# Values' projection partly accumulated beside the keys' in the opening stage, and the recurrence's head arrays split by token chunk

## The chip, the cores and the metric

The kernel runs on one core of a Trainium2 chip. The time is that of one execution in device microseconds, and the number to compare is the median of a few runs. Five engines run their own instruction queues in order: PE multiplies matrices, DVE, ACT and POOL work on vectors, SP issues transfers. They wait for each other through semaphores.

## What is computed

Two layers of a trunk over 128 context tokens and 1024 latent tokens, 1152 columns in all, with model width 1024.

```python
# every sub-layer: h = x*(1+scale)+shift ; x <- LayerNorm(ALPHA*x + gate*sublayer(h))
def _modulation(cond, w_mod, b_mod):
    return jnp.split(jax.nn.silu(cond) @ w_mod + b_mod, 6, axis=-1)
...
def _attn_conv_project(h, w_in, q_gain, k_gain):
    q, k, v, bg, cg, xi = jnp.split(h @ w_in, EVEN_SPLITS, axis=-1)
    ...
# layer 0: attention (8 query heads, 2 key/value heads) beside
    sc = bg * _dwconv(cg * xi, conv_w)
    return jnp.concatenate([att, sc], axis=-1) @ w_out, k, v
# layer 1: HGRN, 8 heads, per direction and head
def _chunk_scan(q, log_f, k, v, s0):
    ...
        decay = jnp.exp(jnp.where(lower, diff, -jnp.inf))
        scores = jnp.einsum('bhtk,bhsk,bhtsk->bhts', qb, kb, decay)
    ...
# after each of the two: a gated ConvFFN
    u = _dwconv(h @ w_up, conv_w); a, gt = jnp.split(u, 2, axis=-1)
    return (jax.nn.silu(gt) * a) @ w_down
```

## The kernel before, in words

Tokens stand on the free axis in three chunks c = 2, 1, 0 of 384 columns (386 or 388 with the halo). A product of full precision is three matmuls on split operands (`mm3`, L93 to L95: hi·hi, hi·lo, lo·hi).

**Opening stage (L341 to L475).** For each of eight blocks b of the model width, `modulation(b)` loads w_mod (`mr`), ACT and DVE split it (L396, L397), 16 matmuls (L403) fill a small bank `psr`, and DVE writes shift and scale (L412, L414). `modulate(b)` transposes x (L421, banks `psx`), DVE applies shift and scale (`ht`, L424), ACT and POOL split it into `hT` (L427, L428), and nine matmuls per chunk group add block b to the keys' projection in `psk`, three banks. The banks of `psr` and `psx` come from one pool of five.

**Features of attention (L545 on).** j = 4 are the keys, j = 5 the values, j = 0 to 3 the queries. `feature` loads a 512 KB weight and runs 72 matmuls into three banks. ACT copies the banks to `fT` (L549), PE transposes `fT` into token order (L558).

**Conv stage (L617 to L641).** Twelve features f0 to f11, three to each j: cg (ACT), xi times cg (`pr`, DVE L630), bg times the convolution (`sc`, DVE L639). Two triples of PSUM banks take turns, so a feature's first matmul waits until the feature two before it has been read. Between these, DVE adds up the rest of the modulation from w_mod (`macc`, L170 and L172, four instructions to each 512 KB load `mraw`; the ring holds two loads), PE transposes the sums (`mps`), DVE reduces them (L183, L184), and `gate_store` (L235) writes the finished gate `gd` to DRAM from SP's queue.

In these stages a scheduler that simulates the kernel's time line picks the order of each engine's instructions. From the out projection of layer 0 on, the order is as written.

**Recurrence (L1500 to L1720).** For each of eight heads, the tile X holds four arrays of 1152 columns. Its items run over levels lv = 0 to 6 and within each over c = 2, 1, 0. `mixed_keys(lv, c)` copies interleaved halves of X into `km` on ACT (L1624). `level(lv, c)` multiplies `km` by X on PE (L1635), and then POOL and DVE each scale one half of X in place (L1641). The queue of PE puts three or six matmuls of the next head's projections between two items. The last head, from 2268 us on, has less to put there.

Of the kernel before, what the change touches and what calls it, by code (L numbers as in the profile page):

```python
# [80 lines left out]
def build(tc, ins, outs, consts):  # L81
# [263 lines left out]
    def bank(name):  # L345
        return pd.tile([P, 512], F32, tag="d", name=name)

    with ExitStack() as st:
        pd = st.enter_context(tc.tile_pool(name="pdS", reuse_waits="tile", bufs=5, space=PSUM))
        sp = st.enter_context(tc.tile_pool(name="sp", reuse_waits="tile", bufs=1))  # L350
# [33 lines left out]

        psk = pu.tile([P, 3, 512], F32, tag="u", name="psu")
        wm = ins["w_mod"][0].rearrange("(k p) (j f) -> p k j f", p=P, j=6)
        def modulation(b):
# [28 lines left out]
        def modulate(b):  # L416
# [12 lines left out]
            for c in (2, 1, 0):  # L429
                a = 1 + c * OW  # L430
                mm3(psk[:, c, :OW], (wkey[0][:, b, :], wkey[1][:, b, :]), (hT[0].k(b, a, OW), hT[1].k(b, a, OW)),
                    b == 0, b == KT - 1)

        modulation(0)
        load_x(0)
        wkey = wload(wcols(w_in, 512), KT, P)
        for b in range(KT):
            if b + 1 < KT:
                modulation(b + 1)
            if b % 2 == 0 and b < 6:  # L440
                load_x(b // 2 + 1)
            modulate(b)
# [56 lines left out]
    with ExitStack() as st:  # L499
        wk = st.enter_context(tc.tile_pool(name="wk", reuse_waits="tile", bufs=1))  # L500
        st.enter_context(qk)
        pus = [st.enter_context(tc.tile_pool(name="puA2", reuse_waits="tile", bufs=1, space=PSUM)), pu]
        pd = st.enter_context(tc.tile_pool(name="pdA", reuse_waits="tile", bufs=2, space=PSUM))
# [42 lines left out]
        for j in (4, 5, 0, 1, 2, 3):  # L546
            ps = psk if j == 4 else feature(pus[(j + 1) % 2], j * P, OW, 1)
            fT = work([P, SW], "fT")
            nc.scalar.activation(fT.rearrange("p (a b) -> p a b", b=OW), ps[:, :, :OW], AF.Copy)  # L549
            if j == 4:  # L550
# [925 lines left out]
    def first_split(n):  # L1476
# [15 lines left out]
    masks = gs.tile([P, 7, P], U8, name="masks")  # L1492
    m32 = gp.tile([P, 4, NTOK], I32, tag="X", name="m32").rearrange("p a b -> p (a b)")[:, :7 * P].rearrange(
        "p (a b) -> p a b", b=P)
# [32 lines left out]
    def scan_ap(X, a0, a1, c0, n, h):  # L1527

        base = X[:, a0, c0:c0 + n]
        return bass.AP(base.tensor, base.offset,  # L1530
                       [list(base.ap[0]), [2 * h, n // (2 * h)], [(a1 - a0) * NTOK + h, 2], [1, h]])

# [6 lines left out]
    class Head:  # L1539
# [42 lines left out]
        def begin(self):  # L1582
            self.X = persistent("X", [P, 4, NTOK])
            self.sT = persistent("sT", [P, NT, P])
            self.T128 = gp.tile([P, 2, NT], F32, tag="T128", bufs=2, name="T128")
            self.tots = {}
# [5 lines left out]
        def arrays(self, c):  # L1592
            X, fb, q, cols = self.X, self.fb, self.q[c], colsof(c)
            nc.scalar.activation(X[:, 0:4:3, cols], fb[:, :, cols], AF.Identity, bias=one, scale=-1.0)
            nc.gpsimd.tensor_tensor(X[:, QAF, cols], q, fb[:, 0, cols], op=ALU.mult)
            nc.vector.tensor_tensor(X[:, QAB, cols], q, fb[:, 1, cols], op=ALU.mult)
            kk = self.kk[c] = wtile("kk")
            nc.vector.tensor_tensor(kk, X[:, KBF, cols], X[:, KBB, cols], op=ALU.add)

# [21 lines left out]
        def mixed_keys(self, lv, c):  # L1621
            km = self.km[lv, c] = wtile("km")
            hh = 1 << lv
            nc.scalar.copy(km.rearrange("p (n s r) -> p n s r", s=2, r=hh),  # L1624
                           scan_ap(self.X, KBF, KBB, c * 384, 384, hh))

        def level(self, lv, c):
            X, cols = self.X, colsof(c)
            hh = 1 << lv
# [3 lines left out]
            for q3 in range(3):  # L1633
                c0 = c * 384 + q3 * P
                mm(ps[:, q3 * P:(q3 + 1) * P], km[:, q3 * P:(q3 + 1) * P], scan_ap(X, QAB, QAF, c0, P, hh),  # L1635
                   start=True, stop=True)
            t4 = self.tots[c][lv].rearrange("p a (n s) -> p a n s", s=2)
            for half, arrs in ((0, slice(0, 2)), (1, slice(2, 4))):
                x = X[:, arrs, cols].rearrange("p a (n s r) -> p a n s r", s=2, r=hh)[:, :, :, half, :]
                eng = nc.vector if half else nc.gpsimd  # L1640
# [6 lines left out]
        def state_at(self, dr, t):  # L1647
            if t == (8 if dr else 1):
                return self.S0[:, dr, :]
            return self.X[:, KBB if dr else KBF, t * P:(t + 1) * P]  # L1650

        def flip(self, dr, c):
            pt = pmt()
            for q3 in range(3):
                t = 3 * c + q3
                nc.tensor.transpose(pt[:, q3 * P:(q3 + 1) * P],
                                    self.X[:, KBB if dr else KBF, t * P:(t + 1) * P], ident)
            kb = wtile("kb")
# [21 lines left out]
        def output(self, c):  # L1680
            po = pst()
            X, V = self.X, shared["V"]
            for q3 in range(3):
                t = 3 * c + q3
                cols = slice(t * P, (t + 1) * P)
                o = po[:, q3 * P:(q3 + 1) * P]
# [438 lines left out]
```

## Time and profile before

| what | value |
|---|---|
| median of 3 runs | 3256.94 us (3255.2 to 3258.32) |
| the profiled execution | 3256.72 us, span 3254.9 us |
| PE busy in the span | 3136.4 us, 96% |
| DVE, POOL, ACT busy | 2247.9, 1422.9, 1288.9 us |

The span is what the trace covers. The time of the execution is 1.8 us longer. PE is the busiest engine, and its idle time is 3254.9 − 3136.4 = 118.5 us.

### The profile page before, as it was taken

To read this page: it belongs to the slowest core of one execution; us is meant where nothing else is said; L and a number is where in the kernel's file an instruction comes from. 1 tells how busy PE (TensorE), PEld (TensorE's weight loads), DVE (VectorE), ACT (ScalarE), POOL (GpSimd) and SP (SyncE) were. 2 spreads that over 40 slices of the span, in tenths; PEclk is the share of its full clock that TensorE was granted. 3 is DMA by queue.
4 is the path that set the end of the run, shared out by engine and by line. 5 is a ranking of instruction groups with operands and counts; after the bars stand their busy time and mean duration, and the time that the engine had idled before them with its cause. 6 is when DMAs were issued, how large, how long until landed. Compare 5 with 4: busy or idle time off the path is not lost. (4 is left out here: it accounts for less than half of the span.)

```text
span 3254.9 us, 48740 instructions
## 1 busy us (share of the span) xinstructions
PE 3136.4 (96%) x19231; PEld 2906.1 (89%) x19231; DVE 2247.9 (69%) x3117; ACT 1288.9 (40%) x2162; POOL 1422.9 (44%) x1011
## 2 busy tenths in 40 slices
PE   7999999899999999998999999999999999999997
PEld 5999888789999998877999999999779999998886
DVE  6778888448988976674466666655556889675356
ACT  4411998333333333115433334333443433335112
POOL 6821242335444534562244333333424545444465
PEclk9999999999999999999999999999999999999999
DMA  7142000322222335541322222211331222225452
GB/s 221 35 136 91 1 1 1 129 85 67 95 91 88 91 119 188 171 154 64 99 83 76 65 68 80 62 50 43 111 122 55 87 91 91 69 82 185 154 169 83
DMA packets 267476, 305.42 MB, mean 94 GB/s; under 512 B 19587, under 2 KB 200015, under 8 KB 267248
## 3 DMA queue, kind: packets, MB, share of 16 engines
q1 hardware_dynamic: 266160, 299.49, 29.0%
q8 instruction: 152, 2.49, 0.3%
q0 software_dynamic: 1088, 2.82, 0.3%
q14 instruction: 76, 0.62, 0.1%
HBM read 237.84 MB, written 64.42 MB: 93 GB/s over the span
## 5 line engine op out<-in xcount | busy, mean ns | idle before, releaser
L1099 POOL TENSOR_TENSOR wlo<-S,whi 128x512 fp32r<-128x512 f32 x152 | 243.1, 1613 | 251.9 <-ACT whi L1098 251.3
L109 POOL TENSOR_TENSOR wlo<-wraw,whi 128x1024 fp32r<-128x1024 f32 x78 | 198.0, 2541 | 203.4 <-ACT whi L108 203.2
L93 PE MATMUL psd<-whi,s 128*128 128x512 f32 x720 | 284.0, 394 | 0.9 <-DVE u L1243 0.9
L95 PE MATMUL psd<-whi,s 128*128 128x512 f32 x720 | 284.0, 394 | 0.0
L94 PE MATMUL psd<-wlo,s 128*128 128x512 f32 x720 | 284.0, 394 | 0.0
L1641 POOL TENSOR_TENSOR X<-X,tot 128x384 f32<-128x384 f32 x144 | 181.4, 1260 | 226.8 <-PE pss L1635 173.7
L1127 DVE SCALAR_TENSOR_TENSOR t<-u,fcw,t 128x1156 f32<-128x1156 f32 x152 | 266.2, 1768 | 13.5 <-ACT t L1122 10.8
L95 PE MATMUL psq<-T,wlo 128*128 128x290 f32 x912 | 271.0, 297 | 0.0
L94 PE MATMUL psq<-T,whi 128*128 128x290 f32 x912 | 270.5, 297 | 0.0
L93 PE MATMUL psq<-T,whi 128*128 128x290 f32 x912 | 270.3, 296 | 0.0
L1099 POOL TENSOR_TENSOR wlo<-wraw,whi 128x512 fp32r<-128x512 f32 x114 | 182.2, 1599 | 173.1 <-ACT whi L1098 157.3
L108 ACT ACTIVATE whi<-wraw 128x1024 fp32r<-128x1024 f32 x130 | 136.8, 1054 | 291.2 <-DMA wraw<-in_ffn_w_down_dram 107.0
L1098 ACT ACTIVATE whi<-S 128x512 fp32r<-128x512 f32 x152 | 92.9, 627 | 323.2 <-DVE S L1077 249.0
L1357 DVE TENSOR_TENSOR y<-y,psd 128x512 f32<-128x512 f32 x144 | 98.0, 684 | 171.9 <-PE psd L95 171.3
L213 DVE SCALAR_TENSOR_TENSOR macc<-mraw,sil,macc 128x512 f32<-128x512 f32 x182 | 191.7, 1092 | 7.1 <-DMA mraw<-in_w_mod_dram 7.1
L93 PE MATMUL psu<-h,whi 128*128 128x388 f32 (+1 forms) x504 | 175.0, 348 | 12.1 <-DVE sc L639 6.9
L1641 DVE TENSOR_TENSOR X<-X,tot 128x384 f32<-128x384 f32 x144 | 102.1, 709 | 113.1 <-PE pss L1635 75.1
L94 PE MATMUL psu<-h,whi 128*128 128x388 f32 (+1 forms) x504 | 174.4, 346 | 2.5 <-POOL h L428 2.5
L1635 PE MATMUL pss<-X,km 128*128 128x128 f32 x1008 | 153.2, 289 | 23.7 <-ACT km L1624 10.3
L93 PE MATMUL psp<-s,whi 128*128 128x384 f32 x480 | 174.7, 364 | 0.0
L95 PE MATMUL psu<-h,wlo 128*128 128x388 f32 (+1 forms) x504 | 173.2, 344 | 0.0
L94 PEld LDWEIGHTS psq<-T,whi 128*128 128x128 f32 x912 | 172.5, 189 | 0.0
(442 smaller groups left out, 10005.2 us busy)
## 6 DMA issues: line engine op xcount, KB each, us to landing
wraw<-in_ffn_w_up_dram SPq DMA_DIRECT2D x88, 512.0 KB, 3.8
mraw<-in_w_mod_dram SPq DMA_DIRECT2D x104, 256.0 KB, 2.8
sraw<-sd SPq DMA_DIRECT2D x40, 578.0 KB, 4.6
wraw<-in_ffn_w_down_dram SPq DMA_DIRECT2D x44, 512.0 KB, 4.1
sd<-t SPq DMA_DIRECT2D x36, 578.0 KB, 3.0
wraw<-in_hgrn_w_in_dram SPq DMA_DIRECT2D x40, 512.0 KB, 4.1
mraw<-in_w_mod_dram SPq DMA_DIRECT2D x28, 512.0 KB, 4.0
wraw<-in_attn_w_in_dram SPq DMA_DIRECT2D x18, 512.0 KB, 3.8
```

Source lines behind the costliest of these rows:

```text
L93: mm(ps, l[0], r[0], start=start, stop=False)
L94: mm(ps, l[0], r[1], start=False, stop=False)
L95: mm(ps, l[1], r[0], start=False, stop=stop)
L108: nc.scalar.activation(hi[:, :n], raw[:, :n], AF.Copy)
L109: (eng or nc.gpsimd).tensor_tensor(lo[:, :n], raw[:, :n], r32(hi[:, :n]), op=ALU.subtract)
L213: nc.vector.scalar_tensor_tensor(acc[:, cond, :], raw, sil[:, cond, k:k + 1], acc[:, cond, :], op0=ALU.mult, op1=ALU.add)
L1098: nc.scalar.activation(hi, src, AF.Copy)
L1099: nc.gpsimd.tensor_tensor(lo, src, r32(hi), op=ALU.subtract)
L1127: nc.vector.scalar_tensor_tensor(t, u[:, :, c0:c0 + HO], taps(p + NF * x)[c0], t, op0=ALU.mult, op1=ALU.add)
L1357: nc.vector.tensor_tensor(y[t][:, cols], y[t][:, cols], ps, op=ALU.add)
L1635: mm(ps[:, q3 * P:(q3 + 1) * P], km[:, q3 * P:(q3 + 1) * P], scan_ap(X, QAB, QAF, c0, P, hh), start=True, stop=True)
L1641: eng.tensor_tensor(x, x, t4[:, :, :, 1 - half].unsqueeze(3).to_broadcast([P, 2, nb, hh]), op=ALU.mult)
```

## The change

Three things are edited. First, `wval`, the values' weight, is loaded right behind the keys', and for every block b the values' chunks 2 and 1 (six matmuls of 386 columns, 48 over the eight blocks) are added up in two banks `psv` of a pool of their own. The feature j = 5 then does chunk 0 alone, 24 matmuls, and ACT copies `psv` to `fTv` ahead of it. Second, the pool of `psr` and `psx` goes from five banks to three, which makes room for the two. Third, X becomes three tiles X0, X1, X2 of 384 columns. No engine gains or loses an instruction except ACT, which has one more.

```diff
+    qv = ExitStack()
+    pv = qv.enter_context(tc.tile_pool(name="puV", reuse_waits="tile", bufs=1, space=PSUM))
     with ExitStack() as st:
-        pd = st.enter_context(tc.tile_pool(name="pdS", reuse_waits="tile", bufs=5, space=PSUM))
+        pd = st.enter_context(tc.tile_pool(name="pdS", reuse_waits="tile", bufs=3, space=PSUM))
...
         psk = pu.tile([P, 3, 512], F32, tag="u", name="psu")
+        psv = pv.tile([P, 2, 512], F32, tag="v", name="psv")
...
                 mm3(psk[:, c, :OW], (wkey[0][:, b, :], wkey[1][:, b, :]), (hT[0].k(b, a, OW), hT[1].k(b, a, OW)),
                     b == 0, b == KT - 1)
+            for c in (2, 1):
+                a = 1 + c * OW
+                mm3(psv[:, c - 1, :OW], (wval[0][:, b, :], wval[1][:, b, :]), (hT[0].k(b, a, OW), hT[1].k(b, a, OW)),
+                    b == 0, b == KT - 1)
...
         wkey = wload(wcols(w_in, 512), KT, P)
+        wval = wload(wcols(w_in, 640), KT, P)
...
+        fTv = wk.tile([P, SW], F32, tag="fT", bufs=2, name="fT")
+        nc.scalar.activation(fTv[:, OW:].rearrange("p (a b) -> p a b", b=OW), psv[:, :, :OW], AF.Copy)
+        qv.close()
         pus = [st.enter_context(tc.tile_pool(name="puA2", reuse_waits="tile", bufs=1, space=PSUM)), pu]
...
-            ps = psk if j == 4 else feature(pus[(j + 1) % 2], j * P, OW, 1)
-            fT = work([P, SW], "fT")
-            nc.scalar.activation(fT.rearrange("p (a b) -> p a b", b=OW), ps[:, :, :OW], AF.Copy)
+            if j == 5:
+                ps, fT = pus[0].tile([P, 3, 512], F32, tag="u", name="psu"), fTv
+                for k in range(KT):
+                    mm3(ps[:, 0, :OW], (wval[0][:, k, :], wval[1][:, k, :]),
+                        (hT[0].k(k, 1, OW), hT[1].k(k, 1, OW)), k == 0, k == KT - 1)
+                nc.scalar.activation(fT[:, :OW], ps[:, 0, :OW], AF.Copy)
+            else:
+                ps = psk if j == 4 else feature(pus[(j + 1) % 2], j * P, OW, 1)
+                fT = work([P, SW], "fT")
+                nc.scalar.activation(fT.rearrange("p (a b) -> p a b", b=OW), ps[:, :, :OW], AF.Copy)
...
-            self.X = persistent("X", [P, 4, NTOK])
+            self.X = [persistent(f"X{c}", [P, 4, 384]) for c in range(3)]
...
             nc.scalar.copy(km.rearrange("p (n s r) -> p n s r", s=2, r=hh),
-                           scan_ap(self.X, KBF, KBB, c * 384, 384, hh))
+                           scan_ap(self.X[c], KBF, KBB, 0, 384, hh))
...
-                mm(ps[:, q3 * P:(q3 + 1) * P], km[:, q3 * P:(q3 + 1) * P], scan_ap(X, QAB, QAF, c0, P, hh),
+                mm(ps[:, q3 * P:(q3 + 1) * P], km[:, q3 * P:(q3 + 1) * P], scan_ap(X, QAB, QAF, q3 * P, P, hh),
                    start=True, stop=True)
...
-                x = X[:, arrs, cols].rearrange("p a (n s r) -> p a n s r", s=2, r=hh)[:, :, :, half, :]
+                x = X[:, arrs, :].rearrange("p a (n s r) -> p a n s r", s=2, r=hh)[:, :, :, half, :]
```

The change also moves rows that it does not name. The order is shown at three places, as the built programs have it.

**PE at the end of the opening stage, before.** `psu_132` is the keys' bank group, and `psu_859` that of the values' feature j = 5, which PE mixes with the keys' last block.

```order
L94 MATMUL psu_859<-h11_95,whi_855 128x386
L95 MATMUL psu_859<-h01_93,wlo_856 128x386
L94 MATMUL psu_132<-h11_95,whi_176 128x386
L95 MATMUL psu_132<-h01_93,wlo_177 128x386
L93 MATMUL psu_132<-h01_93,whi_176 128x386
L93 MATMUL psu_859<-h00_92,whi_855 128x386
L94 MATMUL psu_859<-h10_94,whi_855 128x386
L95 MATMUL psu_859<-h00_92,wlo_856 128x386
L94 MATMUL psu_132<-h11_95,whi_176 128x386
L95 MATMUL psu_132<-h01_93,wlo_177 128x386
L93 MATMUL psu_859<-h00_92,whi_855 128x386
L94 MATMUL psu_859<-h10_94,whi_855 128x386
```

The same place after the change: `psu_135` is the keys', `psv_136` the values' two banks, `psu_914` the values' chunk 0.

```order
L95 MATMUL psv_136<-h01_93,wlo_187 128x386
L93 MATMUL psv_136<-h01_93,whi_186 128x386
L94 MATMUL psu_135<-h11_95,whi_180 128x386
L95 MATMUL psu_135<-h01_93,wlo_181 128x386
L93 MATMUL psu_135<-h01_93,whi_180 128x386
L94 MATMUL psv_136<-h11_95,whi_186 128x386
L95 MATMUL psv_136<-h01_93,wlo_187 128x386
L94 MATMUL psu_135<-h11_95,whi_180 128x386
L95 MATMUL psu_135<-h01_93,wlo_181 128x386
L93 MATMUL psu_914<-h00_92,whi_186 128x386
L94 MATMUL psu_914<-h10_94,whi_186 128x386
L95 MATMUL psu_914<-h00_92,wlo_187 128x386
```

The values' chunks now run through all eight blocks, and their chunk 0 starts only when the last matmul into `psv` has been issued.

**DVE in the conv stage around the second `sc`, before.** `pr` opens the stretch, and L184 is what `gate_store` waits for.

```order
L630 TENSOR_TENSOR pr<-psu,cg 128x1164
L183 TENSOR_REDUCE mods<-mps 128x4 x2
L170 TENSOR_SCALAR macc<-mraw,sil 128x512 x2
L184 TENSOR_TENSOR mods<-mods,colA 128x4 x2
L633 SCALAR_TENSOR_TENSOR yv<-pr,colB,yv 128x1158
L172 SCALAR_TENSOR_TENSOR macc<-mraw,sil,macc 128x512 x2
L634 SCALAR_TENSOR_TENSOR yv<-pr,colB,yv 128x1158
L172 SCALAR_TENSOR_TENSOR macc<-mraw,sil,macc 128x512 x8
L639 TENSOR_TENSOR sc_1676<-psu,yv 128x1158
L172 SCALAR_TENSOR_TENSOR macc<-mraw,sil,macc 128x512 x4
```

After the change the reduction L183 and L184 stands further down among the sums:

```order
L183 TENSOR_REDUCE mods<-mps 128x4 x2
L172 SCALAR_TENSOR_TENSOR macc<-mraw,sil,macc 128x512
L170 TENSOR_SCALAR macc<-mraw,sil 128x512
L172 SCALAR_TENSOR_TENSOR macc<-mraw,sil,macc 128x512
L651 SCALAR_TENSOR_TENSOR yv<-pr,colB,yv 128x1158
L170 TENSOR_SCALAR macc<-mraw,sil 128x512
L184 TENSOR_TENSOR mods<-mods,colA 128x4 x2
L172 SCALAR_TENSOR_TENSOR macc<-mraw,sil,macc 128x512
L652 SCALAR_TENSOR_TENSOR yv<-pr,colB,yv 128x1158
L172 SCALAR_TENSOR_TENSOR macc<-mraw,sil,macc 128x512 x5
L657 TENSOR_TENSOR sc_1682<-psu,yv 128x1158
L172 SCALAR_TENSOR_TENSOR macc<-mraw,sil,macc 128x512 x8
```

From the stage's start, the second `sc` has 60 instructions of `macc` ahead of it before and 56 after, which is 15 and 14 loads.

**SP in the same stretch, before.** The first row here issues loads 11 to 14.

```order
L160 DMA mraw<-in_w_mod_dram 128x2x512 x4
L100 DMA wraw<-in_attn_w_in_dram 128x8x128
L235 DMA gd_83<-mods 128x8x1 x2
L160 DMA mraw<-in_w_mod_dram 128x2x512 x3
L100 DMA wraw<-in_attn_w_in_dram 128x8x128
```

After the change the first row issues loads 10 to 13, and load 14 is the single one below it.

```order
L160 DMA mraw<-in_w_mod_dram 128x2x512 x4
L100 DMA wraw<-in_attn_w_in_dram 128x8x128
L160 DMA mraw<-in_w_mod_dram 128x2x512
L235 DMA gd_83<-mods 128x8x1 x2
L160 DMA mraw<-in_w_mod_dram 128x2x512 x2
L100 DMA wraw<-in_attn_w_in_dram 128x8x128
L160 DMA mraw<-in_w_mod_dram 128x2x512 x2
```

In both orders 14 loads stand ahead of `gd`. The load that the second `sc` needs last was behind `gd` and is now ahead of it.

**PE in the last head of the recurrence, before.** These are the level matmuls with the semaphores that they wait for; rows of other matmuls between them are left out.

```order
L1635 MATMUL pss_20908<-X_14568,km_20894 128x128 [waits Pool_49]
L1635 MATMUL pss_20908<-X_14568,km_20894 128x128 x2
L1635 MATMUL pss_20920<-X_14568,km_20906 128x128 [waits Pool_49]
L1635 MATMUL pss_20920<-X_14568,km_20906 128x128 x2
L1635 MATMUL pss_20937<-X_14568,km_20918 128x128 [waits DVE_49]
L1635 MATMUL pss_20937<-X_14568,km_20918 128x128 x2
```

After the change:

```order
L1652 MATMUL pss_20916<-X1_14575,km_20902 128x128 [waits Activation_49]
L1652 MATMUL pss_20916<-X1_14575,km_20902 128x128 x2
L1652 MATMUL pss_20928<-X0_14574,km_20914 128x128 [waits Activation_49]
L1652 MATMUL pss_20928<-X0_14574,km_20914 128x128 x2
L1652 MATMUL pss_20945<-X2_14576,km_20926 128x128 [waits Activation_49]
L1652 MATMUL pss_20945<-X2_14576,km_20926 128x128 x2
```

The order is the same. Each group waits for ACT alone, where it waited for POOL's or DVE's update of X by the item before it, which belongs to another chunk.

## Rows read from the trace of the kernel before

**Rows 1.** The page, each engine's busy us, share of the span, instructions.

```profile
PE 3136.4 (96%) x19231; PEld 2906.1 (89%) x19231; DVE 2247.9 (69%) x3117; ACT 1288.9 (40%) x2162; POOL 1422.9 (44%) x1011
```

**Rows 2.** Windows: length, busy us of PE, PEld, DVE, ACT, POOL, PEclk, DMA, GB/s.

```profile
17.70:53.60 35.90, 28.87 (x177) 20.87 (x177) 26.61 (x40) 20.84 (x35) 20.82 (x19) 0.95 1.13 315
53.60:83.00 29.40, 29.04 (x189) 26.81 (x190) 19.53 (x48) 14.08 (x30) 21.82 (x30) 1.00 0.28 79
...
238.50:262.10 23.60, 16.69 (x82) 16.44 (x81) 18.34 (x29) 2.11 (x3) 2.34 (x1) 0.78 0.66 193
...
2268.00:2312.00 44.00, 35.22 (x219) 31.09 (x219) 30.31 (x51) 17.07 (x32) 26.64 (x21) 0.96 0.29 89
```

**Rows 3.** PE's waits in the whole span: total us, times, longest.

```profile
PE pss L1635 <- ACT km L1624: 10.3, 11, 1.2
PE pss L1635 <- POOL X L1641: 9.7, 14, 1.7
PE psu L93 <- DVE sc L639: 6.9, 1, 6.9
PE psr L403 <- ACT mhi L396: 6.8, 4, 3.2
...
PE psu L94 <- POOL h L428: 2.5, 4, 1.5
...
PE pss L1635 <- DVE X L1641: 2.1, 6, 0.5
...
PE psu L93 <- DVE pr L630: 2.0, 1, 2.0
```

**Rows 4.** PE's time line: first and last of 28 matmul starts of j = 5.

```profile
75.02 0.33 PE L93 MATMUL psu<-h,whi 128*128 128x386 f32 x1
...
79.77 0.34 PE L93 MATMUL psu<-h,whi 128*128 128x386 f32 x1
```

**Rows 5.** ACT's time line: the keys' copy out of PSUM.

```profile
75.48 1.12 ACT L549 ACTIVATE fT<-psu 128x1158 f32<-128x1158 f32 x1
```

**Rows 6.** DVE's time line: the last block's four `ht`.

```profile
65.60 2.03 DVE L424 TENSOR_SCALAR ht<-psx,s,mods 128x384 f32<-128x384 f32 x4
```

**Rows 7.** DMA issues from 0 to 70 us: count, KB each, median us to landing.

```profile
wraw<-in_attn_w_in_dram SPq DMA_DIRECT2D x5, 512.0 KB, 6.5
```

**Rows 8.** PE's time line in the conv stage: the features f6 and f7 start.

```profile
225.46 0.45 PE L93 MATMUL psu<-h,whi 128*128 128x388 f32 x1 [2.00 <-DVE pr L630]
...
246.28 0.66 PE L93 MATMUL psu<-h,whi 128*128 128x388 f32 x1 [6.91 <-DVE sc L639]
```

**Rows 9.** Windows of the features f7 and f8, columns as in Rows 2.

```profile
246.20:262.10 15.90, 15.82 (x74) 15.81 (x75) 14.25 (x24) 0.13 (x1) 0.00 (x0) 0.80 0.75 229
262.70:275.60 12.90, 12.90 (x76) 12.90 (x75) 12.87 (x19) 1.63 (x3) 3.08 (x2) 1.00 0.33 102
```

**Rows 10.** DVE's time line in the conv stage ahead of the second `sc`.

```profile
228.79 3.54 DVE L172 SCALAR_TENSOR_TENSOR macc<-mraw,sil,macc 128x512 f32<-128x512 f32 x2
...
242.12 2.74 DVE L172 SCALAR_TENSOR_TENSOR macc<-mraw,sil,macc 128x512 f32<-128x512 f32 x4 [5.80 <-DMA mraw<-in_w_mod_dram]
244.78 1.35 DVE L639 TENSOR_TENSOR sc<-psu,yv 128x1158 f32<-128x1158 f32 x1
```

**Rows 11.** DMA issues from 160 to 275 us, columns as in Rows 7.

```profile
mraw<-in_w_mod_dram SPq DMA_DIRECT2D x24, 512.0 KB, 4.0
...
gd<-mods SPq DMA_DIRECT2D x2, 4.0 KB, 10.9
```

**Rows 12.** PE's time line: the first level matmul of the second head.

```profile
1677.72 1.25 PE L1635 MATMUL pss<-X,km 128*128 128x128 f32 x6 [1.15 <-ACT km L1624]
```

**Rows 13.** POOL's time line, one update of X in the last head.

```profile
2284.91 1.28 POOL L1641 TENSOR_TENSOR X<-X,tot 128x384 f32<-128x384 f32 x1 [0.62 <-ACT km L1624]
```

**Rows 14.** PE's time line behind that update.

```profile
2286.25 0.94 PE L1635 MATMUL pss<-X,km 128*128 128x128 f32 x6 [1.26 <-POOL X L1641]
```

**Rows 15.** POOL's groups by shape in the last head, 2268 to 2312 us.

```profile
L1641 POOL TENSOR_TENSOR X<-X,tot 128x384 f32<-128x384 f32 x18 | 22.4, 1244 | 11.8 <-PE pss L1635 6.9 <-ACT km L1624 4.1 <-ACT h L1727 0.6
```

More of the change, by code (lines that the diff above doesn't have):

```diff
@@ L1492, in build @@
     masks = gs.tile([P, 7, P], U8, name="masks")
-    m32 = gp.tile([P, 4, NTOK], I32, tag="X", name="m32").rearrange("p a b -> p (a b)")[:, :7 * P].rearrange(
+    m32 = gp.tile([P, 4, 384], I32, tag="X0", name="m32").rearrange("p a b -> p (a b)")[:, :7 * P].rearrange(
         "p (a b) -> p a b", b=P)
@@ L1530, in scan_ap @@
         return bass.AP(base.tensor, base.offset,
-                       [list(base.ap[0]), [2 * h, n // (2 * h)], [(a1 - a0) * NTOK + h, 2], [1, h]])
+                       [list(base.ap[0]), [2 * h, n // (2 * h)], [(a1 - a0) * 384 + h, 2], [1, h]])
     def colsof(c):
@@ L1592, in arrays @@
         def arrays(self, c):
[L1593 to L1596, printed above, removed]
+            X, fb, q, cols = self.X[c], self.fb, self.q[c], colsof(c)
+            nc.scalar.activation(X[:, 0:4:3, :], fb[:, :, cols], AF.Identity, bias=one, scale=-1.0)
+            nc.gpsimd.tensor_tensor(X[:, QAF, :], q, fb[:, 0, cols], op=ALU.mult)
+            nc.vector.tensor_tensor(X[:, QAB, :], q, fb[:, 1, cols], op=ALU.mult)
             kk = self.kk[c] = wtile("kk")
-            nc.vector.tensor_tensor(kk, X[:, KBF, cols], X[:, KBB, cols], op=ALU.add)
+            nc.vector.tensor_tensor(kk, X[:, KBF, :], X[:, KBB, :], op=ALU.add)
         def totals(self, c):
@@ L1624, in mixed_keys @@
             nc.scalar.copy(km.rearrange("p (n s r) -> p n s r", s=2, r=hh),
-                           scan_ap(self.X, KBF, KBB, c * 384, 384, hh))
+                           scan_ap(self.X[c], KBF, KBB, 0, 384, hh))
         def level(self, lv, c):
-            X, cols = self.X, colsof(c)
+            X = self.X[c]
             hh = 1 << lv
@@ L1633, in level @@
             for q3 in range(3):
-                c0 = c * 384 + q3 * P
-                mm(ps[:, q3 * P:(q3 + 1) * P], km[:, q3 * P:(q3 + 1) * P], scan_ap(X, QAB, QAF, c0, P, hh),
+                mm(ps[:, q3 * P:(q3 + 1) * P], km[:, q3 * P:(q3 + 1) * P], scan_ap(X, QAB, QAF, q3 * P, P, hh),
                    start=True, stop=True)
@@ L1649, in state_at @@
                 return self.S0[:, dr, :]
-            return self.X[:, KBB if dr else KBF, t * P:(t + 1) * P]
+            return self.X[t // 3][:, KBB if dr else KBF, t % 3 * P:(t % 3 + 1) * P]
         def flip(self, dr, c):
@@ L1654, in flip @@
             for q3 in range(3):
-                t = 3 * c + q3
                 nc.tensor.transpose(pt[:, q3 * P:(q3 + 1) * P],
-                                    self.X[:, KBB if dr else KBF, t * P:(t + 1) * P], ident)
+                                    self.X[c][:, KBB if dr else KBF, q3 * P:(q3 + 1) * P], ident)
             kb = wtile("kb")
@@ L1681, in output @@
             po = pst()
-            X, V = self.X, shared["V"]
+            X, V = self.X[c], shared["V"]
             for q3 in range(3):
                 t = 3 * c + q3
-                cols = slice(t * P, (t + 1) * P)
+                cols = slice(q3 * P, (q3 + 1) * P)
                 o = po[:, q3 * P:(q3 + 1) * P]
```

## The prediction, as it was made before the result

> **What bounds the kernel now.** I read the page first. PE is busy for 3136.4 of 3254.9 us [rows 1], so PE's queue is the kernel, and an edit is worth what it does to the 118.5 us in which PE stands still, or to the clock at which PE runs. The windows say where the idle time lies [rows 2]: 35.90 − 28.87 = 7.0 us in the opening's first part (17.7 to 53.6 us), 0.4 us up to 83 us, 6.9 us in the part of the conv stage from 238.5 us on, and 44.00 − 35.22 = 8.8 us in the last head of the recurrence. The waits name what ends them [rows 3]. In the opening it is mostly ACT's and DVE's splitting of w_mod, behind loads that come late. In the conv stage it is two waits on DVE, of 2.0 and 6.9 us. In the recurrence it is ACT's `km` with 10.3 us, POOL's update of X with 9.7 and DVE's with 2.1.
>
> A difference of 0.2% (6.5 us here) is about what a measurement can tell from no change. The profiled execution took 3256.72 us, 0.2 us under the median of the runs shown, so a sum made against it holds for the median too.
>
> **The change, part 1: X in three tiles.** Before, an item's X is part of one tile, so the level matmul of chunk 1 waits for POOL's update of chunk 2, which is the item just before it. The order shown says this outright: the group waits for POOL, and after the change for ACT alone, whose `km` of the same chunk was released three items earlier. The trace shows the price: POOL's update starts at 2284.91 and takes 1.28 us [rows 13], and PE, idle for 1.26 us, starts at 2286.25 [rows 14]. What goes is every wait of `pss` on X: 9.7 + 2.1 = 11.8 us [rows 3]. What stays is the wait on `km` at each head's start, 1.15 us [rows 12], where ACT is late with other work.
>
> What is late next in the last head? POOL needs 1.244 us per update [rows 15], and 21 items in 44 us leave 2.1 us for one. Without its idle time and at full clock PE would need about 34.4 us for them (35.22 less about 0.8 for the clock of 0.96 [rows 2]), 1.64 us per item. That is still more than POOL's 1.24. One chunk's own circle (matmuls 0.94, update 1.28, then `km`, for which I allow 0.6, with about 0.3 for each of three hand-overs: 3.7 us) fits into three items, 4.9 us. So PE is the bound there again. The clock was 0.96 with these pauses, and I count 0.8 back. I give back 0.7 for hand-overs on `km` in the last head. **Term: −12** (bounds −9, if a quarter comes back as waits on `km`, and −14.4, if `km`'s waits inside the last head shrink by 2).
>
> **Part 2: the conv stage, which the diff does not name.** The scheduler gives another order there. In the trace the feature f7 starts at 246.28 after 6.91 us [rows 8], waiting for the second `sc`. DVE did that one at 244.78, behind a sum that had waited 5.80 us for its load [rows 10]. That load is the 15th, issued behind `gd`, whose two stores carry 4 KB each and land only after 10.9 us, where a 512 KB load takes 4.0 [rows 11]. After the change the second `sc` needs 14 loads, all issued ahead of `gd`. So the wait for the late load falls on sums behind `sc`. The clock falls as well after the 6.91 us: the window of f7 lasts 15.90 us at 0.80, that of f8 12.90 at 1.00 [rows 9]. Less the 0.1 us by which f7's window begins before its first matmul, 2.9 us hang on it. With the 2.0 us ahead of f6 [rows 8], where DVE came late with `pr`, 2.0 + 6.9 + 2.9 = 11.8 us are to be had.
>
> I followed DVE's new order by hand, with 2.74/4 = 0.685 us for a sum, 2.2 more where POOL's weight split runs beside it (3.54 us for two sums, which otherwise take 1.37), and 1.35 us for `pr` and `sc` [rows 10]. PE is ready for f6 at 225.46 − 2.00 = 223.5 [rows 8]; the `pr` that it waits for then ends at about 220.7. PE is ready for f7 at 246.28 − 6.91 − 2.0 = 237.4; the second `sc` ends at 236.3. Two features later, at 237.4 + 2 × 12.9 = 263.2, f9 needs the third `pr`, which now takes up the delay of the late load: 260 to 262. A later `sc` or transpose of a sum comes out 1 to 3 us late, for which I give back 2.3. **Term: −9.5** (bounds 0, if the wait turns up again in the same size, and −12).
>
> **Part 3: the opening.** PE does the same matmuls, 48 of them earlier: 48 × 0.176 = 8.4 us (27 steps from 75.02 to 79.77 us, so 0.176 for one [rows 4]). Six stand behind each block's keys, about 1.06 us per block, in a stretch that has 7.0 us of idle time. They take up only waits that come behind them in PE's queue and that have another cause than the block itself: those on `mhi`, 6.8 us with the start [rows 3], but not the 2.5 us on POOL's `h`, which stand ahead of the matmuls. I take 3.5 to 4 us as filled. Costs: (a) `wval` comes first now, and 512 KB at the window's 315 GB/s [rows 2] put 1.7 us ahead of the w_mod loads behind it; the DMA engines are full there (1.13), but each later load gets as much back, so I take 0.5. (b) With three banks the next `psr` waits until a `psx` has been read; DVE's four `ht` of a block take 2.03 us [rows 6], and most of that lies behind the 15 matmuls of keys and values. I take 0.5, with 0 and 14 (seven blocks × 2.03) as the ends. (c) The chunk 0 of the values goes into banks that ACT must first empty: 1158 columns took 1.12 us [rows 5], so 772 take about 0.75; with the hand-over 1 us in which PE has nothing else in its queue. Filled 4, lost 2: **term −2** (bounds −6, if all waits on the split go, and +12, if the far end of (b) holds; half of it is a rival below).
>
> Weight loads: 6.5 us to land [rows 7], and the order of the next three is the same, with one ring slot more in use until the values are done; nothing is late by that.
>
> **Features of j = 5 on.** The evictions and transposes of keys and values move closer together. POOL is the fuller engine there, and PE had next to no idle time. **Term −0.5** (bounds −3, 0).
>
> Sum: −12 − 9.5 − 2 − 0.5 = −24, so 3256.7 − 24 = **3233 us**.
>
> **The rivals.**
> - *The conv wait stays* in another place: the late load behind `gd` now holds the third `pr` or a transpose of the sums, and PE pauses as long, with the fall of the clock. For it: DVE is busy for nearly all of f8, 12.87 of 12.90 us [rows 9], so it catches up slowly. Against it: 24 sums, 16.4 us, lie between the second `sc` and the third `pr`, against 25.8 us of PE's work. Then the 9.5 are lost: 3233 + 9.5 = 3242.5 us.
> - *Three banks are too few*: `psr` waits for half of a block's `ht`, 1.0 us in seven blocks, 7 us in all, and the 2 gained are lost too: 3233 + 9 = 3242 us. For it: `psx` takes three banks for each block, all there are. Against it: 15 matmuls per block are 2.6 us of cover, and no row of before shows a wait for one of the five banks. A rule of the Trainium skill speaks for this rival: Perfetto Trace Analysis, Identifying Performance Opportunities (Optimization Strategy), says that a gap that repeats on the engine that should be full can mean too little SBUF or PSUM for the next tile. By that rule the sum would be that of this case, by the rows it is the forecast.
> - *X in three tiles does nothing*: `km` on ACT or the copies behind it on DVE set the same pace, and the 11.8 us come back under the name of `km`. For it: `km` is already the larger wait [rows 3]. Against it: ACT is busy for 17.07 of 44 us in the last head [rows 2], and nearly all its waits on `km` elsewhere are the seven head starts. 3233 + 12 = 3245 us.
> - *Slower*: the ring of two loads is the brake in the conv stage. If each load must wait for its forerunner's sums and lands 4.0 us later [rows 11], four loads to a feature take 16 us against 12.9 of PE's work [rows 9]. PE then pauses 3.1 us per feature and loses about 2.9 at the clock. Over the five features from f7 on that is 30 us, and the 9.5 are lost: 3233 + 39.5 = 3272 us. It decides from the point where loads follow each other by more than 3.2 us with four to a feature. Against it: 24 loads were spread over 115 us before, 4.8 us for one, without this effect outside of `gd`.
>
> **How the numbers follow.** The forecast has 0.62, with its own range 3226 to 3240 (errors of about 3 us in part 1, 3 in part 2 and 4 in part 3, added as independent ones, are 5.8). The conv wait that stays has 0.17, too few banks 0.10, X without effect 0.07, slower 0.04. The range that leaves out no more than 2 in 10 reaches from the forecast's low end into the three middle cases, 3225 to 3246 us. Faster by over 0.2% means under 3250.4: the forecast and nearly all of the three middle cases, 0.92. Within 0.2%: two of the middle cases together, 0.05. Slower: 0.03.
>
> **What the profile after should show.** `pss` waits for X at no place, and the time from the last head's start to its end is about 35 to 37 us in place of 44. The conv stage has no pause of PE over 3 us, and f7 runs at a clock of 1.00, in 12.9 us. The opening's idle time up to j = 0 is about 5.5 us in place of 7.4, with a wait of about 1 us on the copy of `psv`. After the recurrence nothing changes but the offset. The forecast is wrong if PE waits in the opening for `psx` or `psr`, if a `sc`, `pr` or `mods` wait of over 5 us stands in the conv stage, or if waits on `km` grow by more than 3 us.

## The result and the profile after

The changed kernel takes **3233.43 us** (median of 4 runs, 3233.18 to 3233.95) beside 3257.18 us for the kernel before: a ratio of 0.9929, 95% interval 0.9913 to 0.9945. The forecast was 3233. The sum was right, but two of its terms were not, and their errors happened to cancel. So that the number came out is luck, and this part is about where each microsecond went.

The page of the changed kernel answers to [rows 1]: busy us, share, instructions.

```profile
PE 3128.1 (97%) x19231; PEld 2905.1 (90%) x19231; DVE 2248.6 (70%) x3117; ACT 1284.5 (40%) x2163; POOL 1413.4 (44%) x1011
```

PE's waits in the changed kernel answer to [rows 3].

```profile
PE pss L1652 <- ACT km L1642: 11.7, 13, 1.2
PE psu L93 <- ACT cg L643: 6.8, 1, 6.8
PE psr L406 <- ACT mhi L399: 6.0, 2, 4.5
...
PE psr L406 <- DVE mlo L400: 4.0, 5, 1.0
...
PE psu L93 <- DVE pr L648: 2.1, 1, 2.1
...
PE psu L94 <- POOL h L431: 0.9, 2, 0.5
```

No level matmul waits for X any more, and the 6.9 us on `sc` are gone. In their place stands a wait of 6.8 us on ACT's `cg`, which no step of the prediction named.

Windows of the changed kernel, columns as in [rows 2]: the opening, the stretch around that wait, and the last head.

```profile
17.70:53.60 35.90, 32.23 (x201) 25.45 (x201) 25.15 (x41) 20.10 (x33) 21.40 (x19) 1.00 1.01 293
...
168.11:181.70 13.59, 6.84 (x24) 6.84 (x24) 9.09 (x16) 4.15 (x6) 7.56 (x7) 0.62 0.37 116
...
2252.90:2289.20 36.30, 32.66 (x219) 30.37 (x219) 35.68 (x53) 17.77 (x33) 22.28 (x21) 1.00 0.34 107
```

In the first window PE's idle time fell from 7.0 to 3.7 us, but the window's left edge cuts a wait of 4.47 us that ends at 18.58 us. From the span's start to the same matmul inside j = 0 (at 90.10 us before and 87.95 after), the idle time fell by 1.7 us, from 19.6 to 17.8, and the clock rose from 0.98 to 1.00. The windows, before and then after:

```profile
0.00:90.10 90.10, 70.53 (x429) 57.44 (x430) 56.64 (x116) 42.96 (x73) 57.23 (x72) 0.98 0.71 200
```

```profile
0.00:87.95 87.95, 70.11 (x429) 57.61 (x430) 51.99 (x115) 44.11 (x74) 56.32 (x67) 1.00 0.73 211
```

Around 175 us the granted clock is 0.62 over 13.6 us, a mean of the two levels (1.2 and 2.4 GHz) after PE stood still. The last head takes about 36 us.

Sums of idle time don't show where an execution gains. For that I counted PE's matmuls from the end of its queue and compared the start of the same matmul in two traces. The table gives start before minus start after, in us, so a step between two lines is what that stretch gained. "Again" is a second profile of the changed kernel (e10); the other columns are experiments below. All stand against the one profile of before.

| first matmul of (in the first line, one inside j = 0) | before | after | after, again | e1: X alone | e2: opening alone | e7: gate late | e9: both cures |
|---|---|---|---|---|---|---|---|
| inside j = 0, at 90 us | 90.10 | +2.15 | +3.16 | −0.09 | +5.69 | −0.84 | +3.86 |
| f0 | 142.95 | +1.13 | +2.14 | −0.09 | +4.67 | −0.81 | +3.89 |
| f3 | 183.27 | −7.06 | −4.89 | −0.07 | −3.53 | −0.82 | +3.33 |
| f8 | 262.70 | +5.09 | +6.29 | +0.94 | +8.63 | +8.79 | +11.42 |
| attention | 318.32 | +1.18 | +2.48 | +0.93 | +4.79 | +8.82 | +11.44 |
| out projection | 588.11 | +3.00 | +4.17 | +0.95 | +6.61 | +8.92 | +13.63 |
| recurrence | 1583.26 | +3.14 | +4.92 | +0.81 | +6.65 | +8.29 | +12.88 |
| last head | 2268.10 | +14.26 | +16.04 | +11.93 | +6.63 | +6.65 | +23.74 |
| behind the last head | 2313.21 | +22.85 | +24.64 | +20.53 | +6.91 | +6.27 | +33.12 |
| the end | 3236.10 | +23.12 | +22.37 | +18.93 | +6.91 | +5.78 | +33.14 |

The recurrence gave 22.85 − 3.14 = 19.7 us and not 12: 11.1 in the first seven heads and 8.6 in the last. The conv stage gave 1.18 − 1.13 = 0 and not 9.5: it lost 8.2 us up to f3, won 12.2 from f3 to f8 and lost 3.9 behind it.

### The profile page after: what moved, and what is told of

Its sections match the earlier page's. It is cut to its first block, busy times and chain, and to the rows that moved or that the text cites. A ratio compares the mean times of both kernels' runs of the same rounds, so it can differ in the third digit from the quotient of the medians.

```text
span 3231.8 us, 48746 instructions
## 1 busy us (share of the span) xinstructions
PE 3128.1 (97%) x19231; PEld 2905.1 (90%) x19231; DVE 2248.6 (70%) x3117; ACT 1284.5 (40%) x2163; POOL 1413.4 (44%) x1011
## 5 line engine op out<-in xcount | busy, mean ns | idle before, releaser
L1658 POOL TENSOR_TENSOR X<-X,tot 128x384 f32<-128x384 f32 x144 | 168.7, 1171 | 225.9 <-PE pss L1652 211.1
L93 PE MATMUL psu<-h,whi 128*128 128x388 f32 (+1 forms) x488 | 171.6, 352 | 12.9 <-ACT cg L643 6.8
L1658 DVE TENSOR_TENSOR X<-X,tot 128x384 f32<-128x384 f32 x144 | 111.2, 772 | 88.3 <-PE pss L1652 86.8
L94 PEld LDWEIGHTS psq<-T,whi 128*128 128x128 f32 x912 | 172.2, 189 | 0.0
L95 PEld LDWEIGHTS psq<-T,wlo 128*128 128x128 f32 x912 | 172.2, 189 | 0.0
L93 PEld LDWEIGHTS psq<-T,whi 128*128 128x128 f32 x912 | 172.0, 189 | 0.0
L93 PE MATMUL psp<-h,whi 128*128 128x384 f32 x480 | 172.0, 358 | 0.0
```

What stands on the lines that cost most here:

```text
L93: mm(ps, l[0], r[0], start=start, stop=False)
L94: mm(ps, l[0], r[1], start=False, stop=False)
L95: mm(ps, l[1], r[0], start=False, stop=stop)
L1658: eng.tensor_tensor(x, x, t4[:, :, :, 1 - half].unsqueeze(3).to_broadcast([P, 2, nb, hh]), op=ALU.mult)
```

## The experiments

### The recurrence: what a wait of PE costs

**e1** is the kernel before with X in three tiles and nothing else (the diff's last part, from `self.X` on).

> The kernel before with X in three tiles and nothing else; the opening and the conv stage keep their order. Theory (each wait of the level matmuls on X costs its idle time and about 0.26 us more when the matmuls start again, with the last head's half-clock stretch): the recurrence gives 19.7 us, so 3237.3 us, and PE waits for km alone there. Rival (a wait costs the idle time that the waits view shows, 12 us): 3245 us. In both the conv stage keeps its waits of 2.0 and 6.9 us.

It took 3238.95 us, ratio 0.9944 (0.9929 to 0.9959), 18.1 us under before; PE's waits name `km` alone, with 11.7 us in 13 times. The table gives 20.53 − 0.81 = 19.7 us for the recurrence, the same as in both profiles of the changed kernel. The 12 us of idle time are too little.

Where the rest lies is seen at one ordinary stall of the second head. PE's time line of the kernel before, three starts in a row (the last matmul ahead, the level's group, the first one behind):

```profile
1701.77 0.34 PE L95 MATMUL psp<-s,wlo 128*128 128x384 f32 x1
1702.37 0.94 PE L1635 MATMUL pss<-X,km 128*128 128x128 f32 x6 [0.26 <-POOL X L1641]
1703.06 0.42 PE L93 MATMUL psp<-s,whi 128*128 128x384 f32 x1
```

The same three in the changed kernel:

```profile
1695.19 0.34 PE L95 MATMUL psp<-s,wlo 128*128 128x384 f32 x1
1695.37 0.83 PE L1652 MATMUL pss<-X,km 128*128 128x128 f32 x6
1695.95 0.42 PE L93 MATMUL psp<-s,whi 128*128 128x384 f32 x1
```

From first to third start it is 1.29 us before and 0.76 after, a difference of 0.53 us, of which the row shows 0.26 as idle. The other 0.27 stand in two places. A row ends 0.34 us after its start, but in an undisturbed row of matmuls the next starts after 0.18: the idle time counts from the modelled end, so 0.16 us of each stall are hidden under the matmul ahead. And the group itself takes 0.69 us from its start to the next in place of 0.58. The Trainium skill, Perfetto Trace Analysis, Tensor Engine Instruction (MATMUL, LD_WEIGHTS), says that the profiler estimates a matmul's end from the instruction's size; 0.34 shown against 0.18 between starts agrees.

The other stalls of this kind cost the same on top. The first seven heads have 17 stalls on X of 0.14 us and more, with 5.9 us of idle time in all. Counted from start to start between the same matmuls of both traces, they cost 10.5 us, each of them 0.26 to 0.28 more than its idle time.

**e4** joins chunks 1 and 2 in one tile again, so that only chunk 1's waits remain.

```diff
-                       [list(base.ap[0]), [2 * h, n // (2 * h)], [(a1 - a0) * 384 + h, 2], [1, h]])
+                       [list(base.ap[0]), [2 * h, n // (2 * h)], [(a1 - a0) * X.ap[1][0] + h, 2], [1, h]])
...
-            self.X = [persistent(f"X{c}", [P, 4, 384]) for c in range(3)]
+            x0, x12 = persistent("X0", [P, 4, 384]), persistent("X1", [P, 4, 768])
+            self.X = [x0, x12[:, :, 0:384], x12[:, :, 384:768]]
```

> The kernel before with X in two tiles, chunk 0 alone and chunks 1 and 2 together, so that chunk 1 still waits for chunk 2 and the other two are free; the order of every engine is that of the split in three. In the trace of before, chunk 1's three waits on X are 3.0 us of idle time, all in the last head, and the other 21 waits 9.3 us. Theory (a wait costs its idle time and 0.26 us at the restart): 21 x 0.26 = 5.5 us more, so 14.8 us and 3242 us. Rival (the idle time is all there is): 9.3 us and 3247.7 us.

It took 3241.04 us, ratio 0.995 (0.9934 to 0.9966): 16.5 us, 1.7 more than the theory's 14.8, and the 9.3 us of idle time alone lie outside the interval. The waits that were to stay are there, of [rows 3]'s 14 on POOL three:

```profile
PE pss L1635 <- POOL X L1641: 2.7, 3, 1.0
```

### The two halves

**e2** is the change without the split of X (the diff's other parts).

> The change without the split of X: values' chunks beside the keys', three banks. Theory (the opening gives 1.9 us, the conv stage's cured wait of 11.8 us is lost again at f2 on ACT's cg and at f9, and the attention's tail gives 2.4): 3253.5 us, with a wait of 6.7 us on cg near 175 us. Rival (the recurrence gave only its 12 us of idle time, so the front of the kernel gave the rest): 3246 us.

It took 3254.06 us, ratio 0.9989 (0.998 to 0.9999). With e1, −18.1 and −3.0 make −21.1 us, against 23.8 for both together; the intervals cover the difference. The waits in the conv stage are those of the changed kernel: 6.73 us on `cg` and 2.04 on `pr`. Its profiled execution, though, gained 5.7 us in the opening, where the changed kernel with the same order gained 2.2 and 3.2, so one profile can't settle a term of 2 us there.

**e3** takes two of the five banks from the kernel before, the part against which a rule had spoken.

```diff
-        pd = st.enter_context(tc.tile_pool(name="pdS", reuse_waits="tile", bufs=5, space=PSUM))
+        pd = st.enter_context(tc.tile_pool(name="pdS", reuse_waits="tile", bufs=3, space=PSUM))
```

> The kernel before with three banks instead of five for psr and psx in the opening, nothing else. Theory (the third bank is free again in time behind the keys' matmuls): 3257 us, within 2 us, and no wait for a bank. Rival (psr waits for the reading of psx in seven blocks): 7 us longer, 3264 us, with waits on ht ahead of psr or psx. The values' matmuls, which give cover in the changed kernel, are missing here, so the true cost there is at most this one.

It took 3259.15 us, ratio 1.0008 (0.9999 to 1.0017). Its trace has one stall on a bank:

```profile
63.94 0.30 PE L421 MATMUL psx<-ident,xq 128*128 128x128 f32 x1 [0.23 <-DVE ht L424]
```

By the interval, three banks without the values' matmuls as cover cost −0.3 to 5.5 us, and 7 lie outside. Perfetto Trace Analysis of the Trainium skill (Optimization Strategy) says that a repeating gap can mean too little PSUM; here no wait on a bank repeats. The profiled execution, at 3262.4 us one of the slowest of its ten, reached the matmul of the table's first line 3.25 us later than before all the same, at a clock of 0.95 up to there (0.98 before).

### The conv stage, first wait: what made the 15th load late

**e5** issues the first gate's stores from ACT's queue in the kernel before.

```diff
-    def gate_store(l, j):
+    def gate_store(l, j, eng=None):
...
-            nc.sync.dma_start(gd[l][j // 3][cond]...
+            (eng or nc.sync).dma_start(gd[l][j // 3][cond]...
...
-        gate_store(0, 2)
+        gate_store(0, 2, nc.scalar)
```

> The kernel before with the first gate's two stores issued from ACT's queue instead of SP's; PE, DVE and POOL keep their order row for row. Theory (the load behind gd is late because it stands behind gd in SP's queue): DVE's wait of 5.8 us and PE's of 6.9 us before f7 go, with 2.9 us of lower clock, so about 3247 us; f6's 2.0 us stay. Rival (gd's pieces of 4 bytes hold the DMA engines themselves, whoever issues them): the load is as late and the time stays at 3257 us. A second rival: ACT waits for mods with gd in its queue, its weight splits come late, and PE waits for those: 3257 us or more.

It took 3255.6 us, ratio 0.9994 (0.9984 to 1.0004): no change, and my theory of the queue fell. The load is as late with `gd` in another queue. DVE's time line there, and three windows (columns as in [rows 2]):

```profile
242.48 0.75 DVE L172 SCALAR_TENSOR_TENSOR macc<-mraw,sil,macc 128x512 f32<-128x512 f32 x1 [8.53 <-DMA mraw<-in_w_mod_dram]
```

```profile
234.00:236.00 2.00, 2.00 (x13) 2.00 (x13) 0.00 (x0) 0.00 (x0) 2.00 (x1) 1.00 0.98 39
236.00:238.00 2.00, 2.00 (x13) 2.00 (x12) 0.00 (x0) 0.00 (x0) 0.20 (x1) 1.00 0.54 14
...
240.00:242.00 2.00, 0.00 (x0) 0.00 (x0) 0.00 (x0) 0.24 (x1) 1.64 (x1) 1.00 0.84 243
```

From 234 to 236 us the DMA engines are 98% busy and move 39 GB/s. But it is not `gd`'s pieces that they are busy with there. The DMA view has those from 228 to 231 us, 2080 packets in ACT's queue; from 234 to 236 it has 38 packets, none under 2 KB:

```profile
q10 hardware_dynamic: 2080, 0.01, 37.6%
...
DMA packets 38, 0.08 MB, mean 39 GB/s; under 512 B 0, under 2 KB 0, under 8 KB 38
```

So the 38 are the load's own, at 16 × 2.00 × 0.98 / 38 = 0.83 us each. `gd`'s two stores, though their packets are over by 231 us, land 11.4 us after their issue (the median), at 238.3 and 239.5 us. Once they have landed, from 240 to 242 us, a nearly equal share of 0.84 moves 243 GB/s. The load is slow, then, as long as `gd` has not landed. Through what the two get in each other's way, no view shows.

The Trainium skill, DMA: Bandwidth & Descriptors, Issuing engines are not separate DMA queues, says that transfers run on the same 16 DMA engines and interleave there, whichever engine started them. e5 agrees, as the move to ACT's queue left the load as late as before.

**e7** leaves the stores in SP's queue, but ties them to the end of the conv stage.

```diff
-    def gate_store(l, j):
+    def gate_store(l, j, late=None):
...
+            src = mods[:, l, cond, j * KT:(j + 1) * KT]
+            if late is not None:
+                gcopy = cst.tile([P, KT], F32, name=f"gcopy{cond}")
+                nc.vector.scalar_tensor_tensor(gcopy, late, 0.0, src, op0=ALU.mult, op1=ALU.add)
+                src = gcopy
...
-        gate_store(0, 2)
+        gate_store(0, 2, sc32[:, 3, 0:KT])
```

> The kernel before with the first gate's stores behind the whole conv stage: DVE copies the gate together with zero times the last sc, so that SP issues gd after it; PE, ACT and POOL keep their order row for row, and DVE has two small instructions more at the stage's end. Theory (gd's 2048 pieces of 4 bytes hold the DMA engines, whichever queue they come from, and the 15th load shares the engines with them): the load lands in time, DVE's wait of 5.8 us, PE's 6.9 us before f7 and the 2.9 us of lower clock go, f6's 2.0 us stay: 3247 us. Rival (the ring of two loads is the brake, gd only happens to lie there): the load stays late, 3257 us.

It took 3250.23 us, ratio 0.9978 (0.9968 to 0.9987). DVE no longer waits ahead of the second `sc`, and PE's stall before f7 is 1.25 us on another copy:

```profile
233.27 5.57 DVE L172 SCALAR_TENSOR_TENSOR macc<-mraw,sil,macc 128x512 f32<-128x512 f32 x8
238.76 1.35 DVE L644 TENSOR_TENSOR sc<-psu,yv 128x1158 f32<-128x1158 f32 x1
```

```profile
240.26 0.41 PE L93 MATMUL psu<-h,whi 128*128 128x388 f32 x1 [1.25 <-ACT cg L630]
```

The table gives 8.82 + 0.81 = 9.6 us for the conv stage, as expected; 3 us of them went again later in this execution. So `gd` was the cause (e7), and not by its place in SP's queue (e5).

In the changed kernel the late load still comes, but behind `sc`, as the prediction had it. DVE's time line there:

```profile
239.94 1.35 DVE L657 TENSOR_TENSOR sc<-psu,yv 128x1158 f32<-128x1158 f32 x1
250.55 5.39 DVE L172 SCALAR_TENSOR_TENSOR macc<-mraw,sil,macc 128x512 f32<-128x512 f32 x8 [9.26 <-DMA mraw<-in_w_mod_dram]
```

DVE stands for 9.26 us, and at f9 it is late by 2.12 us:

```profile
272.68 0.48 PE L93 MATMUL psu<-h,whi 128*128 128x388 f32 x1 [2.12 <-DVE pr L648]
```

### The conv stage, second wait: `cg` at f2

f2 needs the banks of f0, which ACT empties with `cg`. In the kernel before that copy ran just in time: it ended at 170.24, and f2 started at 170.56. Before, and then after, ACT's time line:

```profile
90.71 0.49 ACT L575 ACTIVATE qn<-pst 128x384 f32<-128x384 f32 x1 [5.46 <-POOL t L597]
...
169.12 1.12 ACT L625 ACTIVATE cg<-psu 128x1164 f32<-128x1164 f32 x1
```

```profile
94.38 1.06 ACT L108 ACTIVATE whi<-wraw 128x1024 fp32r<-128x1024 f32 x1 [10.68 <-PE psu L94]
95.35 1.12 ACT L567 ACTIVATE fT<-psu 128x1158 f32<-128x1158 f32 x1
96.36 0.48 ACT L593 ACTIVATE qn<-pst 128x384 f32<-128x384 f32 x1
...
173.47 0.31 ACT L628 ACTIVATE qtok<-qn 128x128 f32<-128x128 f32 x1 [4.76 <-DVE qn L603]
173.69 1.12 ACT L643 ACTIVATE cg<-psu 128x1164 f32<-128x1164 f32 x1
```

After the change `cg` stands behind a copy (`qtok`) that waits for the last query's chain on DVE and POOL, and that chain is 4.6 us later. It began to be late at the third group of keys, `qn` at 96.36 in place of 90.71, now queued behind a weight split that waits for the end of j = 0. PE's row at f2 in the changed kernel:

```profile
174.86 0.69 PE L93 MATMUL psu<-h,whi 128*128 128x386 f32 x1 [6.75 <-ACT cg L643]
```

**e6** takes the one copy ahead of `cg` off ACT.

```diff
                     if c == 0:
-                        nc.scalar.activation(dst[:, 0, :], qn[:, 0:P], AF.Copy)
+                        if j == 3:
+                            nc.vector.tensor_copy(dst[:, 0, :], qn[:, 0:P])
+                        else:
+                            nc.scalar.activation(dst[:, 0, :], qn[:, 0:P], AF.Copy)
```

> The changed kernel with one copy of ACT, the last query feature's context rows into qtok (128x128), done by DVE instead; PE keeps its order. Theory (f2's wait of 6.75 us is ACT's cg standing behind that copy, which waits for DVE's chain): cg runs some 5 us earlier, PE waits for 1.8 us or less and keeps its clock, and 6 to 8 us go: 3226 us. Rival (the chain of DVE and POOL behind the queries is late as a whole and pr, which DVE does behind it, holds PE next): the wait comes back at f3 or f4 and the time stays at 3232 to 3234 us.

It took 3233.78 us, so nothing was won. The wait at f2 shrank as expected, and the rival was right in its time all the same: DVE is late with the chain too. It isn't `pr` that holds PE, though, but DVE's sums ahead of the first transposes.

```profile
169.74 0.45 PE L93 MATMUL psu<-h,whi 128*128 128x386 f32 x1 [1.70 <-ACT cg L646]
...
199.63 0.47 PE L181 MATMUL mps<-ident,macc 128*128 128x128 f32 x1 [4.12 <-DVE macc L172]
```

**e8** works on the chain's beginning: eight loads of tables and caches go from POOL's queue to SP's.

```diff
-        nc.gpsimd.dma_start(ctab, consts["ctab"])
-        nc.gpsimd.dma_start(stab, consts["stab"])
+        nc.sync.dma_start(ctab, consts["ctab"])
+        nc.sync.dma_start(stab, consts["stab"])
...
-            nc.gpsimd.dma_start(ck[:, a], ins[src][0, 0].rearrange("(t p) h d -> p t (h d)", p=P))
+            nc.sync.dma_start(ck[:, a], ins[src][0, 0].rearrange("(t p) h d -> p t (h d)", p=P))
```

> The changed kernel with the eight loads of tables, gains and caches issued by SP's queue instead of POOL's, about 4.6 us of POOL's time. The scheduler then puts the third group of keys ahead of the weight split in ACT's queue, as before the change, and gd again ahead of the load that the second sc needs. Theory (f2's wait of 6.75 us comes from the query chain being 4.7 us late, which began at that third group): the chain ends near 170 us, f2 starts without a wait over 1.5 us, and 9.4 us go; the wait before f7 returns with some 10 us: 3234 us in all. Rival (the chain is late because POOL ends its opening work 4.3 us later, whatever stands in ACT's queue): f2 waits as long, f7 too: 3243 us.

It took 3233.84 us, as expected for two effects against each other. The third group of keys runs at 87.68, PE doesn't wait at f2 at all, and the wait before f7 is back:

```profile
242.11 0.66 PE L93 MATMUL psu<-h,whi 128*128 128x388 f32 x1 [7.03 <-DVE sc L657]
```

So the chain behind the queries is what f2 waited for. e8 takes 4.6 us of work from POOL and restores ACT's order in one, so it doesn't tell which of the two had made the chain late.

**e9** has the edits of e8 and e7 on the changed kernel.

> The changed kernel with both edits, the POOL loads on SP's queue and the gate's stores behind the conv stage. If both theories hold, neither f2 nor f7 waits, and no half-clock stretch is left in the conv stage: 3222 to 3224 us, under both kernels. If gd is not the cause: 3234 us. If the query chain stays late: 3232 us.

It took 3225.38 us, ratio 0.9904 (0.9888 to 0.9921). What is left of PE's waits on DVE in the conv stage is short, and the clock from f0 to the attention is 1.00 (0.96 in the changed kernel, 0.97 before):

```profile
222.49 0.45 PE L93 MATMUL psu<-h,whi 128*128 128x388 f32 x1 [2.00 <-DVE pr L653]
...
237.66 0.42 PE L93 MATMUL psu<-h,whi 128*128 128x388 f32 x1 [1.27 <-DVE sc L662]
```

Both kernels once more, on one chip:

> The changed kernel once more, beside the next one on the same chip: 3233 us, within 2.

> The changed kernel with POOL's loads on SP's queue and the first gate's stores behind the conv stage, once more: 3225 us, 8 us under the changed kernel. If the earlier difference was chance between chips or runs, within 3 us of it.

They took 3233.5 us (0.9925, 0.9911 to 0.9939) and 3227.77 us (0.991, 0.9896 to 0.9924). The version with both cures is 6 to 8 us under the changed kernel by the medians of the two pairs of runs, and the fastest of this study. On this one chip it is 5.7 us where 8 were expected. Part of that lies in the opening, where e11's profile reached the matmul of the table's first line 1.31 us later than before, and e9's 3.86 earlier.

## Why the prediction was right, point by point

**Part 1, X in three tiles: right mechanism, mis-sized.** The term was −12 and measured −19.7. The idle time went as forecast: 23.7 us in front of the level matmuls before, 11.7 after, 12.0 less. The claim that PE is the bound in the last head again held: 36.3 us at a clock of 1.00, and `km`'s waits grew by 1.4 us. The step that failed is "what goes is every wait of `pss` on X: 11.8 us": a wait costs more than the idle time in its row. In the first seven heads, which gained 11.1 us, 17 stalls with 5.9 us of idle time cost 10.5. The last head gained 8.6: 6.0 us of idle time, and the clock, 0.96 before and 1.00 after. For the clock I had counted 0.8 us; 0.04 of its 45.1 us would be 1.8, as an estimate.

**Part 2, the conv stage: near in number, half shown in mechanism.** f3 to f8 gained 12.2 us for the 11.8 counted, and 3.9 in place of the 2.3 to be given back went at f9, where the third `pr` came late: a term of −8.2 for −9.5. But the new order is not all that gained these 12.2 us. DVE came later than I had worked out: the second `pr`, put at 220.7, ended at 226.2 us, and the second `sc`, put at 236.3, at 241.3. A PE that was ready for f6 at 223.5 and for f7 at 237.4, as I had it, would have waited for both. It waited for neither because it had lost 7 us by f3 and came to f7 only at 243.91:

```profile
224.81 1.35 DVE L648 TENSOR_TENSOR pr<-psu,cg 128x1164 f32<-128x1164 f32 x1
```

```profile
243.91 0.42 PE L93 MATMUL psu<-h,whi 128*128 128x388 f32 x1
```

No run has the new order with f2 on time, since e8 and e9 change the order again; what the order gives by itself stays open. The reason for the late load was half right as well. Its wait did fall behind `sc`, but its place behind `gd` in SP's queue is not what made it late (e5): `gd`'s stores being under way is, whichever queue they come from (e5 and e7).

**Features of j = 5 on: the step that failed.** "POOL is the fuller engine there, and PE had next to no idle time. Term −0.5 (bounds −3, 0)." From 90 us to f3 the changed kernel lost 9.2 us, far outside. I had looked at what PE waits for inside the stage, where it waits for nothing. What counted was the chain of ACT, DVE and POOL that runs behind the queries into the conv stage. It had 0.3 us to spare at f2. I had read neither that row nor ACT's order at the third group of keys. The profile after was to show no pause of PE over 3 us in the conv stage, and it has one of 6.75 us; the waits that were to refute the forecast were `sc`, `pr` and `mods`, and `cg` was not among them. The first rival, a conv wait that stays in another place, came true in size, but at f2 and by another mechanism than the one I gave it.

**Part 3, the opening: right as far as it can be told.** −2 for the +2.15 and +3.16 of the two profiles at 90 us. The wait on the copy of `psv` was there with 0.55 us, not 1. Loading `wval` first seems to cost more than the 0.5: the second block's first wait on `mhi` went from 3.19 to 4.47 us, and it is 4.5 to 6.1 in the seven profiles with this opening against 3.2 to 4.6 in the six others. No run moved `wval` alone. No PE stall names a bank there. Of the 2.15 us, 1.7 are idle time, and the clock rose too. The profiles with this opening range from −1.3 us (e11, at a clock of 0.96) to +5.7 (e2, at 1.00), so the term isn't known better than that.

**Not in the sum:** 1.8 us between the attention's start and the out projection. It lies in the last 16.2 us of that stretch, which take 14.0 after the change, and it isn't chance from one execution to the next: all seven profiles with the changed opening have 14.0, and of the six others five have 16.2. The sixth is e5, whose PE, DVE and POOL keep the order of before. Names and order of the rows are the same in both cases. One that differs is DVE's last weight split, before and then after:

```profile
582.25 3.37 DVE L109 TENSOR_TENSOR wlo<-wraw,whi 128x1024 fp32r<-128x1024 f32 x1
```

```profile
580.48 2.02 DVE L109 TENSOR_TENSOR wlo<-wraw,whi 128x1024 fp32r<-128x1024 f32 x1
```

What decides between the two isn't shown; no experiment was made on it.

So 7.7 us too little in part 1 and 2 us that stood in no term met 9.7 us too much behind the queries and 1.3 in the rest of the conv stage. Had the recurrence given just the 12 us forecast, the time would have been about 3241 us, above the forecast's own range of 3226 to 3240.

## What to carry to other kernels

Price a stall of PE by the distance between starts, with and without it, not by the idle time in its row. Where a scheduler makes the order, find the copies that end just in time for the engine that bounds, with tenths of a microsecond to spare: a change far ahead of them decides there. And a transfer of a few KB in 4-byte pieces is to be placed like a large one: until it had landed, the load beside it was slow.

## What was not expected of the hardware

Two stores of 4 KB each, in pieces of 4 bytes, took about 11 us to land, and DVE waited 8.53 us for a 512 KB load beside them, though they came from another queue (e5). Their own packets were over some 7 us before they landed. In the meantime the load's packets of 2 KB took 0.83 us each, so that the DMA engines were 98% busy at 39 GB/s (234 to 236 us). A stall of 0.26 us in PE's rows cost 0.53 us.
